# Gated MLP of a hybrid encoder: down-projection operands in rolling groups, token sums on VectorE

## The chip, the core and the metric

The kernel runs on one core of one Trainium2 chip. The metric is device time in microseconds (us) of one execution, and the median of several is quoted. The core's engines each work off their own instruction queue in order: PE (TensorE, with its weight loads, PEld, beside it), DVE (VectorE), ACT (ScalarE), POOL (GpSimd) and SP (SyncE), which here issues the transfers. Semaphores tie them together.

## The reference, cut to what matters

The model is an encoder of two layers on 1024 tokens and 1024 features. Every layer ends in the gated MLP, and the change touches only this:

```python
def _conv_ffn(x, norm_g, w_up, conv_w, conv_b, w_down):
    h = _rmsnorm(x, norm_g)
    up = h @ w_up
    gate, val = up[..., :D_FF], up[..., D_FF:]          # D_FF = 2816
    gate = conv(gate, conv_w) + conv_b                  # depthwise over tokens, width 3
    return (jax.nn.silu(gate) * val) @ w_down

def reference(x, ...):
    for layer in range(2):
        ...                                             # mixing: attention and retention, or gated linear attention
        x = x + _conv_ffn(x, ffn_norm[layer], ...)
    return x
```

Everything is float32. Below, `mid` is the input of the down projection, silu(gate) times val.

## The kernel before

Features lie on the partitions and tokens along the free axis, cut into two halves of 512. A float32 product is made of three matmuls (`mm3`, L350): each operand is split into a rounded high part, which ACT copies (L328), and the rest, which VectorE subtracts (L329). One matmul takes a 128x128 weight and 512 tokens.

**Up projection.** The 2816 features are 22 blocks of 128, i = 0 to 21. The first three go by plain products. Blocks 3 to 21 (`up_fast`) use a scheme of seven products in place of eight over two blocks of rows and the two token halves, each product 12 matmuls into one of four banks b1 to b4. The weights of a block come in two raw pages of 512 KB. VectorE turns them into sums (L1240 to L1243, where L1242 and L1243 write back into the first raw page) and splits them into pages `w` and `wf`; it also adds the banks into u, r and v (L1257). `gated_mid` then makes the convolution taps (L1286), ACT the Silu (L1287), and VectorE two multiplications by v and r (L1289). The raw pages rotate, so that the weights of a block can only be loaded when the splits of the earlier one have read theirs.

**Token sums.** The down projection uses the same scheme over pairs of blocks, for the first 16 blocks (`PAIRED`). From a pair it needs seven operands: three are the halves as they are and four are differences. `Mid.add` makes the four at the end of every odd block, one after the other, on POOL (L1321). All seven go to DRAM; the differences are written at the next block's start (`flush`, L1326).

**Down projection.** `Down` goes over the 16 blocks in two windows of eight (four pairs) and, in each, over four pairs of output blocks m: eight visits of seven products of 12 matmuls. `operands(w, p)` (L1344) loads the two pages (512 KB each, L1352) of operand p of window w through three staging pages `pg` and one `st`, and splits them. All operands of window 0 are loaded while the last up block runs, which is called the seam here, and those of window 1 in visit 3, each after the product that uses the same operand of window 0 last. Weights come six products ahead (`LEAD`; `part`, L1366), with four sums per visit on POOL. Each of the seven results of a visit is added to its accumulator by VectorE (L1417). The six blocks that are not paired are loaded in visit 7 (`rest`) and multiplied plainly after it.

The order on each engine's queue is set by a scheduler from the program's dependences and the rooms of each tag; the transfers all stand in SP's one queue. Thus a load behind one that waits for its page waits too.

The down projection's loop is short:

```python
        for p, (ps, outs) in enumerate(((b1, [u]), (b2, [u]), (b1, [c11]), (b3, [c22]), (b4, [c22]), (b3, [c21]), (b4, [c12]))):
            s = 7 * v + p
            self.product(s, ps, p in (0, 1, 3, 4))
            ...
            self.part(s + LEAD)
            if last and not w:
                self.operands(1, p)
```

Of the kernel before, what the change touches and what calls it, by code (L numbers as in the profile page):

```python
# [17 lines left out]
P = 128  # L18
# [4 lines left out]
H2 = 512  # L23
# [6 lines left out]
PAIRED, WIN, LEAD = 16, 8, 6  # L30
# [37 lines left out]
class Encoder:  # L68
# [1063 lines left out]
    def ffn(self, layer, h, ws, scale, h_gain, xs, gain=None, ahead=None):  # L1132
# [5 lines left out]
        with ExitStack() as stack:  # L1138
# [3 lines left out]
            T = {n: self.pairs(f"h{n}") for n in range(1, 5)}  # L1142
            self.xrooms.pop().close()
            late = stack.enter_context(self.room("left", tt=4))
# [45 lines left out]
    def pairs(self, tag):  # L1190

        pages = [[self.page([P, 2, H2], F32R, tag) for _ in range(2)] for _ in range(2)]
        return [tuple(x[:, j % 2] for x in pages[j // 2]) for j in range(4)]
# [28 lines left out]
    def up_fast(self, layer, i, h, T, mid):  # L1222
# [44 lines left out]
        add(r, b4, r)  # L1267
        yield
# [6 lines left out]
    def gated_mid(self, layer, i, g, v, mid):  # L1275
# [17 lines left out]
class Mid:  # L1293
# [4 lines left out]
    def __init__(self, e):  # L1298
        self.e, self.last, self.late = e, [], []
        self.d = [[[e.waiting() for _ in range(2)] for _ in range(7)] for _ in range(PAIRED // WIN)]  # L1300

    def add(self, i, cv):
        e, nc = self.e, self.e.nc
        if i >= PAIRED:
            d = e.dp.tile([P, 2, H2], F32, name=e.nm("d"))
            nc.sync.dma_start(out=d.rearrange("p h f -> p (h f)"), in_=cv)
            self.last.append(d)
            return
        w, j = divmod(i // 2, WIN // 2)
# [20 lines left out]
class Down:  # L1330
# [4 lines left out]

    A11, S2, A12, S3, S1, A22, S4 = range(7)

    def __init__(self, e, layer, mid):
        self.e, self.nc, self.mid = e, e.nc, mid
        self.w = e.io["ffn_w_down"][layer].rearrange("(k p) f -> p k f", p=P)  # L1340
        self.visits = [(w, m) for w in range(PAIRED // WIN) for m in range(0, NK, 2)]
        self.b, self.parts, self.raw = [{}, {}], {}, {}

    def operands(self, w, p):  # L1344

        e, nc, n = self.e, self.nc, {1: 2, 3: 3, 4: 1, 5: 4}.get(p)
        out = e.pairs(f"h{n}") if n else [tuple(e.page([P, H2], F32R, "hx") for _ in range(2)) for _ in range(4)]
        self.b[w][p] = out
        for a, d in enumerate(self.mid.d[w][p]):
            self.n = getattr(self, "n", -1) + 1  # L1350
            two = e.page([P, 2, H2], tag="st" if self.n % 4 == 3 else "pg")
            nc.sync.dma_start(out=two, in_=d.rearrange("j p f -> p j f"))  # L1352
            if n:
                e.split(two, *(bass.AP(x.tensor, x.offset, [list(x.ap[0]), [H2, 2], [1, H2]]) for x in out[2 * a]))
            else:
                for j in range(2):
                    e.split(two[:, j], *out[2 * a + j])

    def weights(self, v):

        e, nc, (w, m) = self.e, self.nc, self.visits[v]
        wg, wv = (e.page([P, 2, WIN // 2, P], F32, "raw") for _ in range(2))
        for x, c in ((wg, m), (wv, m + 1)):
            src = self.w[:, blk(w, WIN), blk(c)].rearrange("p (j two) f -> p two j f", two=2)
# [8 lines left out]
    def part(self, s):  # L1373

        if s >= 7 * len(self.visits):
            return
# [4 lines left out]
        t = e.page([P, 2, WIN // 2, P], F32R, "wd" if p in (self.S1, self.A22) else "w")  # L1381
# [11 lines left out]
    def product(self, s, ps, first):  # L1393
        t, b = self.parts.pop(s), self.b[self.visits[s // 7][0]][s % 7]
        for j in range(WIN // 2):
            self.e.mm3(ps, (t[:, 0, j], t[:, 1, j]), b[j], first and j == 0, j == WIN // 2 - 1, not first)

    def visit(self, v):
        e, nc, (w, m) = self.e, self.nc, self.visits[v]
        last = m == NK - 2  # L1400
        for i in range(2):
            for hf in range(2):
                if not w:
                    nc.sync.dma_start(out=self.x[m + i][hf], in_=self.xs[2 * (m + i) + hf])
        (c11, c12), (c21, c22) = self.x[m], self.x[m + 1]
        if not w:
            self.u[m] = e.page([P, H2], tag="hx")
        u = self.u[m]
        b1, b2, b3, b4 = (e.bank() for _ in range(4))
        for p, (ps, outs) in enumerate(((b1, [u]), (b2, [u]), (b1, [c11]), (b3, [c22]), (b4, [c22]), (b3, [c21]), (b4, [c12]))):  # L1410
            s = 7 * v + p
            self.product(s, ps, p in (0, 1, 3, 4))
            for x in outs:
                if not w and p == 0:
                    nc.scalar.copy(x, ps)
                else:
                    nc.vector.tensor_tensor(x, ps, x, ALU.add)  # L1417
# [9 lines left out]
    def rest(self, k, n):

        e = self.e
        for k in (k, k + 1):  # L1430
            two = e.page([P, 2, H2], tag="st" if k % 4 == 3 else "pg")
            self.nc.sync.dma_start(out=two, in_=self.mid.last[k])
            parts = [e.page([P, 2, H2], F32R, f"h{n}") for _ in range(2)]
            e.split(two, *parts)
            self.b[1][7 + k] = parts

    def run(self, xs, gain, ahead, stack, ends):
# [10 lines left out]
        for v in range(len(self.visits)):  # L1448
            self.visit(v)
# [241 lines left out]
```

## Time and profile before

| | before |
|---|---|
| median of 3 runs | 2611.17 us (2609.48 to 2611.77) |
| the profiled execution, its own time | 2607.8 us |
| its span in the trace | 2605.7 us |
| mean granted clock of PE | 0.994 |
| busy: PE, VectorE, ACT, POOL | 2511.6, 1811.3, 1202.1, 370.4 us |
| up blocks 4 to 15 by the fast scheme, layer 0 and layer 1 | 878.99 to 1120.69 and 2029.87 to 2277.24 us |
| seam, visits 0 and 1, layer 0 and layer 1 | 1158.77 to 1228.50 and 2339.95 to 2403.09 us |
| last part of visit 1 to visit 4, layer 0 and layer 1 | 1228.50 to 1299.77 and 2403.09 to 2471.99 us |

Times in the trace are counted from the span's start. The windows are cut at starts of products, so that the number of products in them is known from the program: 12 blocks of seven products each in the up windows; 21 and 19 products in the seam's, 23 in each of the last two. The count of matmuls in such a row can be a little short, since a few records are missing. In a row of a timeline, the brackets tell how long the engine was idle ahead of it and what ended this.

### The profile page before, as it was taken

The numbers are of one execution on the slowest core, as the hardware profiler recorded it, in microseconds if no ns is written. First come the engines' busy times: TensorE is split into PE (matmuls) and PEld (weight loads), VectorE is DVE, ScalarE is ACT, GpSimd is POOL, SyncE is SP. The second block draws the span as 40 slices with busy tenths as digits, with TensorE's granted clock in tenths as the row PEclk, the third lists the DMA queues.
The fourth block names the chain that finished last, engine by engine and source line by source line (L and its number), as shares of the span: only waits on it lengthen the run. The fifth ranks groups of instructions, "written<-read, shape, count | busy, mean of one in ns | idle before, by whom it ended". The sixth has DMA issues, their size and how long they took to land. (4 is left out here: it accounts for less than half of the span.)

```text
span 2605.7 us, 33289 instructions
## 1 busy us (share of the span) xinstructions
PE 2511.6 (96%) x12584; PEld 2091.0 (80%) x12584; DVE 1811.3 (70%) x2763; ACT 1202.1 (46%) x2215; POOL 370.4 (14%) x342
## 2 busy tenths in 40 slices
PE   8999999999999999998999999999999999998999
PEld 8989877777887877786788898887787777787787
DVE  6545788788578777777757545658687777777752
ACT  5234767779343333334434455566443333334422
POOL 0000033432001111103330000000001111102330
PEclk9999999999999999999999999999999999999999
DMA  5111100004622233337524121224722222337523
GB/s 192 46 38 42 50 26 9 13 14 154 193 89 89 93 97 101 102 114 236 162 83 134 57 64 42 73 69 133 236 80 97 85 97 97 102 105 250 162 75 120
DMA packets 305686, 262.21 MB, mean 101 GB/s; under 512 B 15788, under 2 KB 240149, under 8 KB 305525
## 3 DMA queue, kind: packets, MB, share of 16 engines
q1 hardware_dynamic: 300917, 251.69, 30.4%
q10 hardware_dynamic: 4608, 8.39, 0.9%
q8 instruction: 99, 1.62, 0.3%
q14 instruction: 62, 0.51, 0.1%
HBM read 189.52 MB, written 70.52 MB: 100 GB/s over the span
## 5 line engine op out<-in xcount | busy, mean ns | idle before, releaser
L350 PE MATMUL mm<-hx,w 128*128 128x512 f32 (+1 forms) x3408 | 828.2, 394 | 11.1 <-ACT wd L328 4.4
L350 PEld LDWEIGHTS mm<-hx,w 128*128 128x128 f32 (+1 forms) x3408 | 635.3, 188 | 150.2 <-ACT hx L1259 3.6
L328 ACT CAST w<-raw 128x512 fp32r<-128x512 f32 (+2 forms) x321 | 255.6, 807 | 449.7 <-PE mm L350 217.6
L329 DVE TENSOR_TENSOR w<-raw,w 128x1024 fp32r<-128x1024 f32 (+2 forms) x271 | 268.1, 994 | 260.8 <-ACT w L328 245.2
L350 PE MATMUL mm<-h,wf 128*128 128x512 f32 x1368 | 339.1, 397 | 29.7 <-DVE hx L1257 24.2
L350 PE MATMUL mm<-w,hx 128*128 128x256 f32 (+1 forms) x2304 | 364.1, 305 | 2.4 <-POOL w L329 1.9
L350 PE MATMUL mm<-h,w 128*128 128x512 f32 x1416 | 336.6, 390 | 0.0
L350 PEld LDWEIGHTS mm<-h,wf 128*128 128x128 f32 x1368 | 259.1, 191 | 94.9 <-DVE hx L1257 34.8
L350 PEld LDWEIGHTS mm<-w,hx 128*128 128x128 f32 x2304 | 307.7, 192 | 21.5 <-POOL w L329 2.9
L350 PEld LDWEIGHTS mm<-h,w 128*128 128x128 f32 x1416 | 264.7, 188 | 54.7
L328 ACT CAST wf<-raw 128x1024 fp32r<-128x1024 f32 x78 | 81.8, 1052 | 186.5 <-DVE raw L1243 173.4
L1321 POOL TENSOR_TENSOR tt<-pg 128x512 f32<-128x512 f32 x16 | 28.2, 1761 | 958.9 <-DVE pg L1289 734.9
L1257 DVE TENSOR_TENSOR hx<-mm,hx 128x512 f32<-128x512 f32 x190 | 129.8, 683 | 13.3 <-PE mm L350 13.3
L350 PE MATMUL mm<-hx,wf 128*128 128x512 f32 x552 | 133.5, 392 | 3.6 <-DVE hx L1257 3.6
L350 PEld LDWEIGHTS mm<-hx,wf 128*128 128x128 f32 x552 | 102.8, 188 | 29.2 <-DVE hx L1257 7.9
L329 DVE TENSOR_TENSOR wf<-raw,wf 128x1024 fp32r<-128x1024 f32 x78 | 95.2, 1222 | 23.8 <-ACT wf L328 23.8
L350 PE MATMUL mm<-h,wd 128*128 128x512 f32 x384 | 95.0, 401 | 12.1 <-DVE xa L1417 6.2
L350 PE MATMUL mm<-hr,hr 128*128 128x512 f32 x336 | 104.2, 404 | 1.4 <-ACT hf L1614 1.4
L350 PEld LDWEIGHTS mm<-h,wd 128*128 128x128 f32 x384 | 73.5, 193 | 30.3 <-issue 8.9
L1287 ACT ACTIVATE pg<-pg 128x1024 f32<-128x1024 f32 x44 | 46.7, 1061 | 107.0 <-DVE pg L1286 106.8
L1286 DVE SCALAR_TENSOR_TENSOR pg<-mm,c,pg 128x512 f32<-128x512 f32 (+1 forms) x100 | 74.1, 748 | 31.1 <-issue 16.9
L1321 POOL TENSOR_TENSOR tt<-pg,tt 128x512 f32<-128x512 f32 x32 | 52.2, 1632 | 293.2 <-DVE pg L1289 293.2
(385 smaller groups left out, 3621.8 us busy)
## 6 DMA issues: line engine op xcount, KB each, us to landing
raw<-in_ffn_w_up SPq DMA_DIRECT2D x88, 512.0 KB
pg<-d SPq DMA_DIRECT2D x52, 512.0 KB
d<-tt SPq DMA_DIRECT2D x64, 256.0 KB
raw<-in_ffn_w_down SPq DMA_DIRECT2D x64, 256.0 KB
d<-pg SPq DMA_DIRECT2D x55, 256.0 KB
raw<-in_ffn_w_down SPq DMA_DIRECT2D x32, 384.0 KB
raw<-in_w_in_odd SPq DMA_DIRECT2D x24, 512.0 KB
raw<-in_w_out_even SPq DMA_DIRECT2D x16, 512.0 KB
```

The source lines that it names most:

```text
L328: self.nc.scalar.copy(hi, src)
L329: return (rest or self.nc.vector).tensor_tensor(lo, src, hi.bitcast(F32), ALU.subtract)
L350: mm = lambda w, x, start, stop: self.nc.tensor.matmul(out, lhsT=w, rhs=x, start=start, stop=stop, skip_group_check=more)
L1257: add = lambda out, x, y: nc.vector.tensor_tensor(out, x, y, ALU.add)
L1286: nc.vector.scalar_tensor_tensor(dst, g[hf][:, src], cw(tap), dst, ALU.mult, ALU.add)
L1287: nc.scalar.activation(cv, cv, AF.Silu)
L1321: nc.gpsimd.tensor_tensor(t, x, y, ALU.subtract)
```

## The change

Three things are changed. The two windows of the down projection become four groups of four blocks (two pairs), of which two are live at a time. The visits are listed as (m, first group, number of groups): the first and the last visit use one group (products of 6 matmuls), the seven between them two (12 matmuls). Group 0 is loaded at the seam, group 1 in visit 0, group 2 in visit 3, group 3 in visit 4; the unpaired blocks in visits 7 and 8. The token sums move from POOL to VectorE and out of `Mid.add`: they are put on a list, and `Mid.step` makes one, called after the second r accumulation and after the Silu of each block. The pages `tt` for them become six in place of four and are closed one block later.

```diff
-PAIRED, WIN, LEAD = 16, 8, 6
+PAIRED, LEAD = 16, 6
+VISITS = [(0, 0, 1), (2, 0, 2), (4, 0, 2), (6, 0, 2), (0, 1, 2), (2, 2, 2), (4, 2, 2), (6, 2, 2), (0, 3, 1)]
...
-            late = stack.enter_context(self.room("left", tt=4))
+            late = stack.enter_context(self.room("left", tt=6))
...
-                    if i == PAIRED:
+                    if i == PAIRED + 1:
+                        while mid.todo:
+                            mid.step()
                         mid.flush()
...
         add(r, b4, r)
+        mid.step()
         yield
...
         nc.scalar.activation(cv, cv, AF.Silu)
+        mid.step()
         for hf, sl in enumerate(halves()):
             nc.vector.tensor_tensor(cv[:, sl], cv[:, sl], v[hf], ALU.mult)
...
-            self.first = two
+            self.first, self.t1 = two, t()
             nc.sync.dma_start(out=at(0), in_=two[0])
+            self.todo.append((self.t1, two[1], two[0], at(4)))
             return
...
-        for t, x, y in ((t1, b12, b11), (t2, b22, t1), (t3, b22, b12), (t4, b21, t2)):
-            nc.gpsimd.tensor_tensor(t, x, y, ALU.subtract)
-        self.late += [(at(p), t) for p, t in ((4, t1), (1, t2), (3, t3), (5, t4))]
+        self.todo += [(t(), two[1], b12, at(3)), (t2, two[1], t1, at(1)), (t(), two[0], t2, at(5))]
+
+    def step(self):
+
+        if self.todo:
+            t, x, y, d = self.todo.pop(0)
+            self.e.nc.vector.tensor_tensor(t, x, y, ALU.subtract)
+            self.late.append((d, t))
...
+    def stage(self, src):
+
+        self.loads += 1
+        two = self.e.page([P, 2, H2], tag="pg" if self.loads % 4 else "st")
+        self.nc.sync.dma_start(out=two, in_=src)
+        return two
+
+    def operands(self, g, p):
+
+        e, n = self.e, {1: 2, 3: 3, 4: 1, 5: 4}.get(p)
+        two = self.stage(self.mid.d[g][p].rearrange("j p f -> p j f"))
...
-        e, nc, (w, m) = self.e, self.nc, self.visits[v]
-        wg, wv = (e.page([P, 2, WIN // 2, P], F32, "raw") for _ in range(2))
+        e, nc, (m, g, n) = self.e, self.nc, VISITS[v]
+        wg, wv = (e.page([P, 2, 2 * n, P], F32, "raw") for _ in range(2))
...
-        for j in range(WIN // 2):
-            self.e.mm3(ps, (t[:, 0, j], t[:, 1, j]), b[j], first and j == 0, j == WIN // 2 - 1, not first)
+        bs = [b for i in range(n) for b in self.b[g + i, s % 7]]
+        for j, b in enumerate(bs):
+            self.e.mm3(ps, (t[:, 0, j], t[:, 1, j]), b, first and j == 0, j == 2 * n - 1, not first)
...
-            if last and not w:
-                self.operands(1, p)
-            if last and w and p in (1, 3, 4):
-                self.rest({1: 0, 3: 2, 4: 4}[p], {1: 2, 3: 3, 4: 1}[p])
+            then = {0: 1, 3: 2, 4: 3}.get(v)
+            if then:
+                self.operands(then, p)
+            if v in (7, 8) and p in (1, 3, 4):
+                self.rest({1: 0, 3: 1, 4: 2}[p] + 3 * (v - 7), {1: 2, 3: 3, 4: 1}[p])
```

VectorE's queue in layer 0, in the block that follows an odd paired block. L1257 (L1260 in the changed program) adds a bank into r, u or v; L1242 and L1243 (L1245 and L1246) write the raw weight page. Before:

```order
L1241 TENSOR_TENSOR raw_8767<-raw_8766,raw_8767 128x512
L329 TENSOR_TENSOR w_8791<-sw_8774,w_8791 128x512
L1257 TENSOR_TENSOR hx_8654<-mm_8651,hx_8653 128x512
L1242 TENSOR_TENSOR raw_8766<-sw_8774,raw_8766 128x512
L1243 TENSOR_TENSOR raw_8766<-raw_8766 128x512
L1257 TENSOR_TENSOR hx_8654<-mm_8652,hx_8654 128x512
L329 TENSOR_TENSOR wf_8784<-raw_8766,wf_8783 128x1024
L1257 TENSOR_TENSOR hx_8655<-mm_8651,hx_8653 128x512
```

The same stretch in the changed program, where L1331 is a token sum:

```order
L1244 TENSOR_TENSOR raw_8763<-raw_8762,raw_8763 128x512
L330 TENSOR_TENSOR w_8785<-sw_8768,w_8785 128x512
L1260 TENSOR_TENSOR hx_8653<-mm_8650,hx_8652 128x512
L1245 TENSOR_TENSOR raw_8762<-sw_8768,raw_8762 128x512
L1331 TENSOR_TENSOR tt_8708<-pg_8694,pg_8557 128x512
L1246 TENSOR_TENSOR raw_8762<-raw_8762 128x512
L1331 TENSOR_TENSOR tt_8705<-pg_8694,tt_8568 128x512
L1260 TENSOR_TENSOR hx_8653<-mm_8651,hx_8653 128x512
L330 TENSOR_TENSOR wf_8778<-raw_8762,wf_8777 128x1024
L1331 TENSOR_TENSOR tt_8709<-pg_8694,tt_8705 128x512
L1260 TENSOR_TENSOR hx_8654<-mm_8650,hx_8652 128x512
```

Three sums of the pair stand here, two of them ahead of the second r accumulation; the fourth, tt_8568, stands between L1245 and L1246 of the block before.

SP's queue at the seam of layer 0. d_7718 to d_7731 are the operands in DRAM: before, d_7718 + 2p and the next hold operand p of window 0; the store into d_10771 is that of up block 20. Before:

```order
L1352 DMA pg_10787<-d_7719 128x2x512
L1366 DMA raw_10900<-in_ffn_w_down 128x4x128 x2
L1366 DMA raw_10901<-in_ffn_w_down 128x4x128 x2
L1352 DMA pg_10848<-d_7720 128x2x512
L1352 DMA pg_10864<-d_7722 128x2x512
L1352 DMA pg_10870<-d_7723 128x2x512
L1306 DMA d_10771<-pg_10761 128x1024
L1352 DMA st_10884<-d_7725 128x2x512
L1352 DMA pg_10880<-d_7724 128x2x512
L1352 DMA pg_10892<-d_7726 128x2x512
L1352 DMA pg_10896<-d_7727 128x2x512
```

The same place in the changed program, where d_7718 + p holds operand p of group 0 and d_7725 + p that of group 1:

```order
L1358 DMA pg_10834<-d_7719 128x2x512
L1387 DMA raw_10862<-in_ffn_w_down 128x2x128 x2
L1387 DMA raw_10863<-in_ffn_w_down 128x2x128 x2
L1358 DMA pg_10840<-d_7720 128x2x512
L1358 DMA pg_10856<-d_7722 128x2x512
L1311 DMA d_10771<-pg_10761 128x1024
L1358 DMA st_10989<-d_7725 128x2x512
L1358 DMA pg_10930<-d_7723 128x2x512
L1358 DMA pg_10936<-d_7724 128x2x512
```

Operand 1 (S2), which was d_7720 behind the down weights, is now d_7719 ahead of them, and the first page of group 1 stands already among the pages of group 0.

SP's queue behind the weights of the next visit, in visit 0. The store into d_10928 is that of the last up block, 21 (that into d_10966 before); xa and xb are the accumulators. Before, the store comes behind all loads of window 0:

```order
L1366 DMA raw_11062<-in_ffn_w_down 128x4x128
L1352 DMA pg_10972<-d_7728 128x2x512
L1352 DMA st_10976<-d_7729 128x2x512
L1352 DMA pg_10988<-d_7730 128x2x512
L1366 DMA raw_11062<-in_ffn_w_down 128x4x128
L1366 DMA raw_11063<-in_ffn_w_down 128x4x128 x2
L1352 DMA pg_10994<-d_7731 128x2x512
L1404 DMA xb_11012<-d_7082 128x512
L1306 DMA d_10966<-pg_10956 128x1024
```

In the changed program:

```order
L1387 DMA raw_11006<-in_ffn_w_down 128x4x128
L1387 DMA raw_11007<-in_ffn_w_down 128x4x128 x2
L1358 DMA pg_11020<-d_7726 128x2x512
L1358 DMA pg_11036<-d_7727 128x2x512
L1311 DMA d_10928<-pg_10918 128x1024
L1426 DMA xb_10958<-d_7082 128x512
L1358 DMA st_11073<-d_7729 128x2x512
L1358 DMA pg_11057<-d_7728 128x2x512
L1358 DMA pg_11089<-d_7730 128x2x512
L1358 DMA pg_11105<-d_7731 128x2x512
```

The last four loads of group 1 stand behind the store of the last up block and one accumulator load.

## Rows read from the trace of the kernel before

**Rows 1.** The page's first part: busy time, share of the span, instructions.
```profile
PE 2511.6 (96%) x12584; PEld 2091.0 (80%) x12584; DVE 1811.3 (70%) x2763; ACT 1202.1 (46%) x2215; POOL 370.4 (14%) x342
```

**Rows 2.** Waits of PE; columns: us in total, times, longest us.
```profile
PE mm L350 <- DVE hx L1257: 27.9, 28, 4.1
```

**Rows 3.** Timeline of PE, blocks without sums: start us, us, what, idle before.
```profile
1120.69 2.88 PE L350 MATMUL mm<-h,wf 128*128 128x512 f32 x12
...
1139.73 1.07 PE L350 MATMUL mm<-h,wf 128*128 128x512 f32 x4
```

**Rows 4.** Timeline of PE: the same product in two blocks with sums, two blocks apart.
```profile
899.18 3.01 PE L350 MATMUL mm<-h,wf 128*128 128x512 f32 x12 [0.97 <-DVE hx L1257]
...
939.55 3.02 PE L350 MATMUL mm<-h,wf 128*128 128x512 f32 x12 [0.85 <-DVE hx L1257]
```

**Rows 5.** Timeline of DVE in a block that follows an odd one.
```profile
916.21 1.78 DVE L329 TENSOR_TENSOR w<-sw,w 128x512 fp32r<-128x512 f32 x1
...
918.52 1.17 DVE L1242 TENSOR_TENSOR raw<-sw,raw 128x512 f32<-128x512 f32 x1
919.72 1.67 DVE L1243 TENSOR_TENSOR raw<-raw 128x512 f32<-128x512 f32 x1
```

**Rows 6.** Timeline of POOL in the same stretch, the first of three.
```profile
915.93 1.52 POOL L1321 TENSOR_TENSOR tt<-pg,tt 128x512 f32<-128x512 f32 x1 [17.95 <-DVE pg L1289]
```

**Rows 7.** Timeline of DVE in two blocks without sums.
```profile
1136.81 0.69 DVE L329 TENSOR_TENSOR w<-sw,w 128x512 fp32r<-128x512 f32 x1
1137.41 0.69 DVE L1257 TENSOR_TENSOR hx<-mm,hx 128x512 f32<-128x512 f32 x1
...
1155.67 0.68 DVE L1257 TENSOR_TENSOR hx<-mm,hx 128x512 f32<-128x512 f32 x1
```

**Rows 8.** Windows: us, busy PE, PEld, DVE, ACT, POOL, PEclk, DMA, GB/s.
```profile
878.99:1120.69 241.70, 233.36 (x1010) 187.92 (x1008) 184.22 (x230) 79.59 (x96) 34.01 (x21) 1.00 0.31 99
2029.87:2277.24 247.37, 234.81 (x1010) 189.01 (x1009) 185.21 (x229) 79.64 (x96) 37.49 (x23) 0.99 0.30 98
1158.77:1228.50 69.73, 61.27 (x253) 49.37 (x252) 55.17 (x71) 33.73 (x50) 19.47 (x12) 0.95 0.73 242
1228.50:1299.77 71.27, 65.35 (x278) 52.62 (x276) 50.32 (x64) 29.02 (x45) 22.09 (x15) 0.98 0.50 161
2339.95:2403.09 63.14, 55.73 (x230) 44.86 (x228) 53.03 (x69) 30.19 (x47) 17.72 (x12) 0.95 0.77 253
2403.09:2471.99 68.90, 63.74 (x278) 51.49 (x276) 50.11 (x64) 29.02 (x45) 20.46 (x15) 1.00 0.49 159
```

**Rows 9.** Timelines of DVE and PE at the first fast block.
```profile
786.10 1.78 DVE L329 TENSOR_TENSOR h<-pp,h 128x512 fp32r<-128x512 f32 x1
...
809.35 0.73 PE L350 MATMUL mm<-h,wf 128*128 128x512 f32 x2 [2.55 <-ACT wf L328]
```

**Rows 10.** Timelines of DVE and PE at the seam and in visit 0.
```profile
1173.48 1.91 DVE L329 TENSOR_TENSOR h<-pg,h 128x1024 fp32r<-128x1024 f32 x1 [1.10 <-ACT h L328]
1175.32 3.42 DVE L1289 TENSOR_TENSOR pg<-pg,hx 128x512 f32<-128x512 f32 x2
...
1179.40 4.60 PE L350 MATMUL mm<-h,wf 128*128 128x512 f32 x12 [4.15 <-DVE hx L1257]
...
1203.19 3.41 PE L350 MATMUL mm<-h,wd 128*128 128x512 f32 x9 [2.83 <-DVE xa L1417]
```

**Rows 11.** Timeline of DVE in visit 3, operand splits with and without POOL's work.
```profile
1257.10 2.31 DVE L329 TENSOR_TENSOR h<-pg,h 128x1024 fp32r<-128x1024 f32 x1
...
1262.23 1.21 DVE L329 TENSOR_TENSOR h<-pg,h 128x1024 fp32r<-128x1024 f32 x1
```

**Rows 12.** Timeline of ACT: the cast of a block's weights, layer 0 and layer 1.
```profile
1145.54 1.05 ACT L328 CAST w<-raw 128x1024 fp32r<-128x1024 f32 x1 [2.06 <-DMA raw<-in_ffn_w_up]
...
2266.32 1.05 ACT L328 CAST w<-raw 128x1024 fp32r<-128x1024 f32 x1 [6.21 <-DMA raw<-in_ffn_w_up]
```

**Rows 13.** Chain that ended last, from 2350 to 2366 us: start us, us, what.
```profile
2356.99 6.54 DMA pg<-d
```

More of the change, by code (lines that the diff above doesn't have):

```diff
@@ L1140, in ffn @@
                 h4 = stack.enter_context(self.room("left", **{f"h{n}": 4}))
-            T = {n: self.pairs(f"h{n}") for n in range(1, 5)}
+            T = {n: [tuple(x[:, j] for x in two) for two in (self.pairs(f"h{n}"), self.pairs(f"h{n}")) for j in range(2)]
+                 for n in range(1, 5)}
             self.xrooms.pop().close()
-            late = stack.enter_context(self.room("left", tt=4))
+            late = stack.enter_context(self.room("left", tt=6))
             with self.room("right", pp=2, wf=2):
@@ L1190, in pairs @@
     def pairs(self, tag):
-        pages = [[self.page([P, 2, H2], F32R, tag) for _ in range(2)] for _ in range(2)]
-        return [tuple(x[:, j % 2] for x in pages[j // 2]) for j in range(4)]
+        return [self.page([P, 2, H2], F32R, tag) for _ in range(2)]
     def block_sums(self, h, j, out):
@@ L1298, in __init__ @@
     def __init__(self, e):
-        self.e, self.last, self.late = e, [], []
-        self.d = [[[e.waiting() for _ in range(2)] for _ in range(7)] for _ in range(PAIRED // WIN)]
+        self.e, self.last, self.todo, self.late = e, [], [], []
+        self.d = [[e.waiting() for _ in range(7)] for _ in range(PAIRED // 4)]
     def add(self, i, cv):
@@ L1340, in __init__ @@
         self.w = e.io["ffn_w_down"][layer].rearrange("(k p) f -> p k f", p=P)
[L1341 to L1357, printed above, removed]
+        self.b, self.parts, self.raw, self.loads = {}, {}, {}, 0
@@ new lines, in stage @@
+    def stage(self, src):
[6 more added lines that the diff above has]
+        two = self.stage(self.mid.d[g][p].rearrange("j p f -> p j f"))
+        if n:
+            pages = e.pairs(f"h{n}")
+            e.split(two, *pages)
+            self.b[g, p] = [tuple(x[:, j] for x in pages) for j in range(2)]
+        else:
+            self.b[g, p] = [tuple(e.page([P, H2], F32R, "hx") for _ in range(2)) for _ in range(2)]
+            for j in range(2):
+                e.split(two[:, j], *self.b[g, p][j])
@@ L1359, in weights, with rest @@
+    def rest(self, k, n):
+        two = self.stage(self.mid.last[k])
+        self.b[k] = self.e.pairs(f"h{n}")
+        self.e.split(two, *self.b[k])
     def weights(self, v):
[L1361 to L1362 removed]
+        e, nc, (m, g, n) = self.e, self.nc, VISITS[v]
+        wg, wv = (e.page([P, 2, 2 * n, P], F32, "raw") for _ in range(2))
         for x, c in ((wg, m), (wv, m + 1)):
[L1364 removed]
+            src = self.w[:, 4 * g:4 * (g + n), blk(c)].rearrange("p (j two) f -> p two j f", two=2)
@@ L1365, in weights @@
             for i in range(2):
                 nc.sync.dma_start(out=x[:, i], in_=src[:, i])
-        s1, s4 = (e.page([P, WIN // 2, P], tag="hx") for _ in range(2))
+        s1, s4 = (e.page([P, 2 * n, P], tag="hx") for _ in range(2))
         nc.gpsimd.tensor_tensor(s1, wv[:, 0], wv[:, 1], ALU.add)
@@ L1398, in visit @@
     def visit(self, v):
[L1399 to L1403, printed above, removed]
+        e, nc, (m, g, n) = self.e, self.nc, VISITS[v]
+        first, last = m not in self.u, g + n == PAIRED // 4
+        if first:
+            for i in range(2):
+                for hf in range(2):
                     nc.sync.dma_start(out=self.x[m + i][hf], in_=self.xs[2 * (m + i) + hf])
-        (c11, c12), (c21, c22) = self.x[m], self.x[m + 1]
@@ L1423, in visit @@
-        if w:
+            if first and p == 0:
+                nc.scalar.copy(x, ps)
+            else:
+                nc.vector.tensor_tensor(x, ps, x, ALU.add)
+            self.part(s + LEAD)
+            then = {0: 1, 3: 2, 4: 3}.get(v)
[3 more added lines that the diff above has]
+                self.rest({1: 0, 3: 1, 4: 2}[p] + 3 * (v - 7), {1: 2, 3: 3, 4: 1}[p])
+        if last:
             for x in (c21, c12, c22):
@@ L1425, in visit @@
                 nc.gpsimd.tensor_tensor(x, x, u, ALU.add)
[L1427 to L1435, printed above, removed]
     def run(self, xs, gain, ahead, stack, ends):
@@ L1447, in run @@
             self.x = [[e.page([P, H2], tag="xt") for _ in range(2)] for _ in range(NK)]
-        for v in range(len(self.visits)):
+        for v in range(len(VISITS)):
             self.visit(v)
```

29 lines of the change are left out of this document (11 added, 18 removed).

## The prediction

> **What bounds the kernel now.** The page's busy shares come first [rows 1]: PE is busy 96% of the span, so time can only come out of the stretches where it waits or runs slowly. The waits of PE come second [rows 2]: the largest entry by far is its wait for VectorE's line L1257, the accumulation of an up block. The third reading is the timeline of PE in two up blocks. A block without sums runs seven products of 12 matmuls, and the A22 products of two such blocks start 19.04 us apart [rows 3], which is 2.72 us per product with no gap. Two blocks with sums take 939.55 − 899.18 = 40.37 us, 2.29 more than 38.08, and both rows name L1257 [rows 4]. The fourth reading is VectorE beside POOL there: a VectorE operation of 128x512 takes 0.69 us in a block without sums [rows 7], but 1.78, 1.17 and 1.67 us where POOL's three subtractions of L1321 run (the first from 915.93 to 917.45) [rows 5, 6]. So POOL's operation makes VectorE's wait, 1.09 + 0.48 + 0.98 = 2.55 us per odd block.
>
> The Trainium skill, "SBUF — State Buffer", section "Who interferes with whom", calls VectorE's second port pair a lock shared with GpSimd, which a VectorE instruction with two SBUF inputs contends for; w<-sw has two such inputs, and its 1.78 us agrees.
>
> VectorE is not full (184.22 of 241.70 us [rows 8]), but it closes a loop: the first r accumulation, L1242, L1243, the split that frees the raw page, the next weights' load, their split, the taps, the multiplications, and the next r accumulation. Without POOL this loop takes 1155.67 − 1137.41 = 18.26 us [rows 7], 0.78 shorter than PE's 19.04; POOL's waits make it longer than PE's time, and PE waits.
>
> The windows [rows 8] give what is lost in all, as elapsed time less products times 2.72: the twelve paired fast blocks of each layer lose 241.70 − 228.48 = 13.2 and 247.37 − 228.48 = 18.9 us (32.1 together). The seam with the first two visits loses 69.73 − 21 × 2.72 = 12.6 and 63.14 − 19 × 2.72 = 11.5 us (24.1). The four-visit window's change loses 71.27 − 23 × 2.72 = 8.7 and 68.90 − 62.56 = 6.3 us (15.0).
>
> **The change part by part.** Matmuls stay the same (8 visits of 84 become 7 of 84 and 2 of 42), as do the loaded operand bytes.
>
> A, the sums in the paired blocks. Removed: 64 subtractions of POOL. Added: 64 of VectorE, 0.60 us each in a row of operations (1136.81 to 1137.41; the 0.69 in the row overlaps the next [rows 7]). By the order, one sum stands in the block after an even one and three in the block after an odd one, although the change asks for two per block. At most three of the four lie in the loop where nothing covers them; one stands where VectorE waits for ACT's cast. A pair then takes 2 × 18.26 + 3 × 0.60 = 38.32 us of loop against PE's 38.08: 0.24 short, 1.4 us over six pairs, or 0.84 and 5.0 us with all four in the loop. The loop starts ahead, so part of this never reaches PE. What stays besides are late weight loads in layer 1: ACT waited 6.21 us for one against 2.06 in an undisturbed block [rows 12], 4.15 late. The 32.1 us leave between 0 and 2 × 5.0 + 4.15 = 14; I take 5, near three sums per pair with part of the lead gone. **−27**, between −32 and −18.
>
> B, the start of the fast blocks. PE waits 2.55 us there for a split weight, and VectorE's splits beside POOL's subtractions take 1.78 instead of 0.69 us [rows 9]. Four such delays (4 × 1.09 = 4.4 us) lie ahead of it in each layer, and three sums (3 × 0.60 = 1.8) come in. 2.5 per layer: **−5**, between 0 and −8.
>
> C, the seam and visits 0 and 1. PE waits 4.15 us at the seam, runs the next 12 matmuls in 4.60 instead of 2.88 us (the stretch's granted clock is 0.95, part of it at the 1.2 GHz level), and waits 2.83 us in visit 0 for an accumulation [rows 10]. Ahead of the seam stand a split of 1.91 us that first waited 1.10 for its page, and two multiplications of 3.42 us [rows 10] beside POOL's work on the down weights. The first group needs half as many operand splits (one of 1.21 less, −1.2); visit 0's POOL operations have half the size, which takes up to 3.42 − 2 × 0.69 = 2.0 and 1.91 − 1.21 = 0.7; and the waited-for load stands ahead of the down weights in SP's order (−1.1). That is up to 5.0 per layer, and with it the slow matmuls (1.7).
> Against this stands the second group, which is loaded in visit 0. That visit is only 7 × 1.36 = 9.5 us long (half of 19.04). VectorE needs 7 × (0.60 for the eviction + 0.60 for the weight + 1.21 for the operand) = 16.9 us there, 7.4 more; but the last of it is wanted in the second half of visit 1's products, 2.72 us apart, and the same seven operands were split in this stretch before. On SP, four of the group's loads stand behind the last store of an up block, which waits for the multiplications, and behind the accumulator loads. Ends: −24 (everything lost here goes) and +15 (7.4 paid in full in both layers). I take 5 + 1.7 less about 3 of lateness per layer, which is nearest to the seam's own rows: **−7**.
>
> D, the change of window. Before, one visit loads and splits 14 pages: 7 × 1.20 + 14 × 1.21 = 25.3 us of VectorE in 19.04 us of PE. After, visits 3 and 4 take seven each: 16.9 us, which fits. POOL's weight subtractions still slow some splits (2.31 against 1.21 [rows 11]), about three per visit, so each visit stands at 16.9 + 3 × 1.10 = 20.2 and can lose 1.2, 2 × 2 × 1.2 = 4.8 in all, and a restart may come with it; of the 15.0 I take **−9**; ends −15 and 0.
>
> E, the ninth visit. Visit 8's products last 1.36 us, about one eviction (0.68) and its handover; seven more evictions per layer. Where VectorE is idle they cost nothing; paid in full, 2 × 7 × 0.68 = 9.5. I take **+1.5**. The weight loads are more and smaller with the same bytes, in stretches where DMA is at most 0.77 busy [rows 8]: zero, up to 2.
>
> Sum against the profiled execution's own 2607.8 us: −27 − 5 − 7 − 9 + 1.5 = −46.5, 2561.3 us. The median of the runs lies 3.4 above that execution, so **2565 us**.
>
> **The rivals.** (1) Partial: all four sums pace the loop and loads come late (A −18, its end, instead of −27), and the second group eats the seam's gain (C 0 instead of −7): 16 worse, 2581 us. For it: the loop has only 0.78 us to spare per block. Against: it has a lead at the start, and one sum stands in a wait.
> (2) Better: every wait named in A to D goes but 3 of A and half of C's: −29 − 8 − 12 − 15 = −64, 2547 us. For it: the unpaired blocks show a PE without gaps. Against: POOL still works in the visits.
> (3) Slower, by one mechanism: the second group's loads go one at a time. A load took 6.54 us from issue to landing on the chain that ended last [rows 13]; with the cast and split of 1.05 + 1.21 that is 8.8 us, seven of them 61.6, and from the last up block's start to the end of visit 0 there are 19.04 + 9.5 = 28.5. PE would wait 33 us per layer: 2607.8 − 27 − 5 − 9 + 1.5 + 66 = 2634, a median of 2638 us. It decides against the change from about 20 us of waiting per layer, one page every 7 us. For it: the loads stand in one in-order queue behind a store that waits. Against: four staging pages can be in flight, and this stretch moves 242 GB/s [rows 8], 2.2 us per 512 KB.
> (4) VectorE saturates: a pair keeps its 40.37 us and the four sums come on top, 4 × 0.60 = 2.4 us per pair, 14 pairs: +34 instead of −27 and B's −5, 2607.8 + 34 − 7 − 9 + 1.5 = 2627, a median of 2631 us. For it: VectorE is the engine that PE waits for. Against: it is busy only 76% of this stretch [rows 8], and the waits for POOL leave it with its work.
> The Trainium skill, "Perfetto Trace Analysis", section "Optimizing Scalar/DVE Operations", says that a saturated VectorE may be relieved by giving work to GpSimd, and that the shared port can spoil this; by its first half this change goes the wrong way and case 4 holds, by its second half A holds. The slowed rows [rows 5] bear out the second.
>
> **How the numbers follow.** Forecast 0.68 (its own range is 2553 to 2577: C's 7 gone and one more of A's or D's moved by 5, either way), partial 0.13, better 0.09, loads one at a time 0.05, VectorE saturated 0.02; the remaining 0.03 lie within 0.2% of no change, about 5 us, which is what a measurement of this kernel can tell from none. The range from 2546 to 2590 holds the first three, less a tail. Faster 0.90, same 0.03, slower 0.07.
>
> **What would show it.** In the changed trace L1245's and L1246's operations should take 0.69 us in every paired block, POOL be idle there, and pairs take 38.1 to 38.5 us. The stretch of twelve blocks should last about 231 us in each layer. The seam should show PE waiting under 3 us, and visits 3 and 4 about 20 us each. The forecast is wrong if PE waits more than 5 us at one place in visit 1 (case 3), or if a pair takes over 39 us without any slowed operation (case 4).

## The result, and the profile after

The changed kernel takes 2572.04 us (2567.66 to 2572.68) against 2610.32 us before: a ratio of 0.985, interval 0.9832 to 0.9867, so it is 38 us faster. The forecast was 2565 us, its range 2546 to 2590. The profiled execution took 2571.87 us, with a span of 2570.0.

The windows of the changed kernel, cut at the same kinds of products as in [rows 8] (us, busy PE, PEld, DVE, ACT, POOL, PEclk, DMA, GB/s). The first two are the twelve up blocks, the third and fifth the seam to the sixth product of visit 1, the fourth and sixth four visits, from the last product of visit 1 to that of visit 5:

```profile
877.25:1105.73 228.48, 228.48 (x1009) 189.25 (x1008) 178.38 (x250) 81.61 (x96) 0.00 (x0) 1.00 0.32 105
2009.84:2239.14 229.30, 229.30 (x1010) 188.77 (x1008) 176.46 (x252) 79.55 (x96) 0.00 (x0) 1.00 0.33 107
1143.81:1198.36 54.55, 50.56 (x213) 40.69 (x212) 47.47 (x66) 30.40 (x46) 15.40 (x11) 0.97 0.74 235
1198.36:1288.69 90.33, 80.44 (x335) 64.53 (x334) 58.31 (x79) 33.61 (x54) 25.97 (x19) 0.96 0.52 167
2301.83:2350.77 48.94, 44.47 (x190) 34.74 (x188) 42.55 (x63) 26.00 (x41) 12.64 (x10) 1.00 0.78 259
2350.77:2440.45 89.68, 80.41 (x336) 64.60 (x334) 58.84 (x80) 33.61 (x54) 27.61 (x20) 0.96 0.52 167
```

Twelve blocks last 228.48 us, to the hundredth what 84 products take without a gap, and VectorE is no busier than before (178.38 against 184.22 us) although it does 20 operations more: the waits for POOL were in that busy time. The four visits hold 28 products, 76.2 us, and last 90.33 and 89.68: there 14.2 and 13.5 us are lost, where the change of window lost 8.7 and 6.3 before. Step by step, in us and in both layers together:

| step | forecast | measured | from |
|---|---|---|---|
| A, up blocks | −27 | −31.3 | 241.70 and 247.37 to 228.48 and 229.30 |
| B, start of the fast blocks | −5 | −7.8 | PE loses 1.6 and 1.5 us, before 4.7 and 6.2 |
| C, seam, visits 0 and 1 | −7 | −10.4 | 54.55 − 17.5 × 2.72 = 6.9 and 48.94 − 15.5 × 2.72 = 6.8, before 12.6 and 11.5 |
| D, visits 2 to 5 | −9 | +12.7 | 14.2 and 13.5 over 28 products each, before 8.7 and 6.3 over 23 |
| E, ninth visit | +1.5 | about 0 | no wait of PE there |

This makes −37; the profiled executions differ by −35.9.

PE's timeline of the changed kernel, the start of the fast blocks and, in layer 0, the longest wait of each of the visits 2 to 5 (in visit 2 with the S1 product ahead of it; a visit's seven products are A11, S2, A12, S3, S1, A22 and S4, in this order):

```profile
809.57 2.79 PE L351 MATMUL mm<-h,wf 128*128 128x512 f32 x11 [0.34 <-DVE wf L330]
...
1211.58 2.88 PE L351 MATMUL mm<-h,wd 128*128 128x512 f32 x12
1218.75 4.62 PE L351 MATMUL mm<-h,wd 128*128 128x512 f32 x12 [4.29 <-DVE xa L1436]
...
1241.74 4.32 PE L351 MATMUL mm<-h,wd 128*128 128x512 f32 x12 [2.04 <-DVE xa L1436]
...
1264.20 3.00 PE L351 MATMUL mm<-h,wd 128*128 128x512 f32 x12 [1.47 <-DVE xa L1436]
...
1285.89 2.97 PE L351 MATMUL mm<-h,wd 128*128 128x512 f32 x12 [1.33 <-DVE xa L1436]
```

The 2.55 us of [rows 9] are 0.34. In each of these visits the A22 product waits for an eviction, that is, for VectorE to add the bank of an earlier product to its accumulator. Visit 2 waits longest, and VectorE splits no operands there (none from 1192.68 to 1229.99 us), so operand splits cannot be the reason. What VectorE did there stands in four timelines of the changed kernel around 1210 us (VectorE, ACT, POOL, and SP, which issues the weight load of visit 3):

```profile
1205.50 0.69 DVE L330 TENSOR_TENSOR w<-raw,w 128x512 fp32r<-128x512 f32 x1 [0.79 <-ACT w L329]
1214.48 1.22 DVE L330 TENSOR_TENSOR w<-raw,w 128x512 fp32r<-128x512 f32 x1 [8.29 <-PE mm L351]
1215.62 0.68 DVE L1436 TENSOR_TENSOR hx<-mm,hx 128x512 f32<-128x512 f32 x1
...
1218.02 0.68 DVE L1436 TENSOR_TENSOR xa<-mm,xa 128x512 f32<-128x512 f32 x1
...
1213.83 1.66 ACT L329 CAST w<-raw 128x512 fp32r<-128x512 f32 x3 [7.87 <-POOL raw L1406]
...
1209.77 1.29 POOL L1389 TENSOR_TENSOR hx<-raw 128x512 f32<-128x512 f32 x1 [9.22 <-DMA raw<-in_ffn_w_down]
1211.14 1.29 POOL L1390 TENSOR_TENSOR raw<-raw,raw 128x512 f32<-128x512 f32 x1
1212.50 1.29 POOL L1406 TENSOR_TENSOR raw<-hx,raw 128x512 f32<-128x512 f32 x1
...
1204.13 0.92 SPq L1387 DMA_DIRECT2D raw<-in_ffn_w_down  x2
```

VectorE stands idle for 8.29 us, with evictions queued; the one that A22 needs begins at 1218.02. Its next operation is a weight split of the *next* visit; the split waits for ACT's cast, the cast for POOL's third sum, POOL for the load, and the load was issued only at 1204.13, when the raw page came free. The row puts VectorE's wait down to PE, but the split needs the cast, and ACT's first cast, begun at 1213.83, is what came last. This is theory W (weights) of the expectations below.

### The profile page after: what moved, and what is told of

It reads as the page before. It is cut to its first block, busy times and chain, and to the rows that moved or that the text cites. A ratio compares the mean times of both kernels' runs of the same rounds, so it can differ in the third digit from the quotient of the medians.

```text
span 2570.0 us, 33323 instructions
## 1 busy us (share of the span) xinstructions
PE 2501.4 (97%) x12584; PEld 2090.5 (81%) x12584; DVE 1793.7 (70%) x2855; ACT 1207.7 (47%) x2229; POOL 264.5 (10%) x286
## 4 chain that ended last, share of the span: by engine, by line
PE 74%; DVE 13%; ACT 5%; DMA 4%; issue 3%; POOL 1%; SPq 0%; POOLq 0%; DVEq 0%; ACTq 0%
PE mm L351 64%; DVE w L330 1%; DVE h L330 1%; ACT w L329 1%; DMA raw<-in_ffn_w_down 1%; PE mr L1104 1%; PE mr L351 1%; PE mr L1541 1%; DVE sr L1597 1%; PE mr L1543 1%; DVE pg L1290 1%; DVE hx L330 1%; PE mr L854 1%; PE mr L1034 1%; PE mr L1596 1%
## 5 line engine op out<-in xcount | busy, mean ns | idle before, releaser
L329 ACT CAST w<-raw 128x512 fp32r<-128x512 f32 (+3 forms) x329 | 257.3, 792 | 421.6 <-PE mm L351 214.2
L330 DVE TENSOR_TENSOR w<-raw,w 128x1024 fp32r<-128x1024 f32 (+3 forms) x279 | 272.3, 980 | 225.9 <-ACT w L329 202.2
L351 PE MATMUL mm<-h,wf 128*128 128x512 f32 x1368 | 329.2, 389 | 0.6 <-DVE wf L330 0.6
L351 PEld LDWEIGHTS mm<-w,hx 128*128 128x128 f32 x2304 | 307.7, 192 | 21.9 <-POOL w L330 3.0
L1389 POOL TENSOR_TENSOR hx<-raw 128x512 f32<-128x512 f32 (+1 forms) x18 | 22.7, 1263 | 1666.2 <-DMA raw<-in_ffn_w_down 1630.2
L1260 DVE TENSOR_TENSOR hx<-mm,hx 128x512 f32<-128x512 f32 x190 | 129.9, 684 | 42.8 <-PE mm L351 42.8
L351 PE MATMUL mm<-h,wd 128*128 128x512 f32 x384 | 99.8, 411 | 17.8 <-DVE xa L1436 9.1
L330 DVE TENSOR_TENSOR wf<-raw,wf 128x1024 fp32r<-128x1024 f32 x78 | 95.4, 1223 | 17.3 <-ACT wf L329 17.3
L351 PE MATMUL mm<-hf,w 128*128 128x512 f32 x384 | 88.8, 392 | 0.0
```

Source lines behind the costliest of these rows:

```text
L329: self.nc.scalar.copy(hi, src)
L330: return (rest or self.nc.vector).tensor_tensor(lo, src, hi.bitcast(F32), ALU.subtract)
L351: mm = lambda w, x, start, stop: self.nc.tensor.matmul(out, lhsT=w, rhs=x, start=start, stop=stop, skip_group_check=more)
L1260: add = lambda out, x, y: nc.vector.tensor_tensor(out, x, y, ALU.add)
```

## Experiments

Ratios are to the kernel before, timed on the same chip in the same session (median 2605.5 to 2606.3 us there).

**e1, the sums alone.** The changed `Mid` and its calls, in the kernel before; windows and visits as they were:

```diff
...
         add(r, b4, r)
+        mid.step()
         yield
...
```

> The kernel before with the token sums on VectorE alone (six tt pages, one sum per step); the down projection keeps its two windows and eight visits. Theory W (weights): the waits of PE in the visits come from the next visit's weights, whose load, POOL sums, cast and split stand ahead of evictions in VectorE's queue, and the operand groups do not touch them; the whole gain is the sums'. Then this kernel lies at 2568 to 2574 us, not slower than the changed kernel (2572), with the up phase free of waits and about 39 us of losses left in seam and visits, as before (21.3 and 17.8 us in the two layers). Theory G (groups help, sums hurt): the rolling groups gain about 14 us in the visits, as predicted, and the moved sums cost as much there; then this kernel lies at 2583 to 2588 us.

Measured: 2568.09 us, ratio 0.9855 (0.984 to 0.9869). From the seam on PE loses 17.3 and 19.9 us in the two layers, where the kernel before lost 21.3 and 17.8. Theory W; G falls. The edit changes two things at once, the engine of the sums and their place (one by one instead of four in a row); which of them gains was not tried apart. The slowed rows [rows 5] and the 0.68 us of the same lines now speak for the engine.

**e2, the groups alone.** The changed kernel with the sums back on POOL:

```diff
...
-        self.todo += [(t(), two[1], b12, at(3)), (t2, two[1], t1, at(1)), (t(), two[0], t2, at(5))]
+        for t, x, y in ((t1, b12, b11), (t2, b22, t1), (t3, b22, b12), (t4, b21, t2)):
+            nc.gpsimd.tensor_tensor(t, x, y, ALU.subtract)
...
```

> The changed kernel with the token sums back on POOL, all four at the end of the odd block, and four tt pages: the rolling groups and nine visits alone. Theory W: nothing is gained, 2609 to 2615 us; the up phase loses its 32 us as before, and seam and visits lose 39 to 42 us. Theory G: 2594 to 2599 us, with under 28 us lost in seam and visits.

Measured: 2607.34 us, ratio 1.0006 (0.9997 to 1.0015). The rolling groups and the nine visits by themselves change nothing in the time. With e1 this puts the whole gain on the sums. But the groups move where PE loses. The windows of this kernel, cut like the last four of the changed kernel's (17.5 and 28 products in layer 0, 15.5 and 28 in layer 1):

```profile
1159.70:1214.99 55.29, 51.09 (x213) 40.58 (x212) 48.90 (x67) 30.43 (x46) 14.79 (x11) 0.97 0.74 247
1214.99:1304.95 89.96, 80.90 (x336) 65.32 (x334) 57.97 (x78) 33.69 (x54) 24.50 (x19) 0.94 0.51 162
2338.43:2388.60 50.17, 44.49 (x190) 34.77 (x188) 44.87 (x64) 26.48 (x42) 14.65 (x11) 1.00 0.77 260
2388.60:2478.00 89.40, 80.88 (x336) 65.55 (x334) 57.96 (x78) 33.71 (x54) 24.36 (x19) 0.94 0.50 163
```

At the seam 7.7 and 8.0 us are lost instead of 12.6 and 11.5, and in the four visits behind it 13.8 and 13.2 instead of 8.7 and 6.3. e1, without the groups, loses 9.8 and 12.1 at the seam and 7.6 and 7.8 behind it.

**e3, weight sums on VectorE.** All four of a visit:

```diff
-        nc.gpsimd.tensor_tensor(s1, wv[:, 0], wv[:, 1], ALU.add)
-        nc.gpsimd.tensor_tensor(wv[:, 0], wg[:, 0], wv[:, 0], ALU.subtract)
+        nc.vector.tensor_tensor(s1, wv[:, 0], wv[:, 1], ALU.add)
+        nc.vector.tensor_tensor(wv[:, 0], wg[:, 0], wv[:, 0], ALU.subtract)
...
-            nc.gpsimd.tensor_tensor(r[p], r[self.S1], r[p], ALU.subtract)
+            nc.vector.tensor_tensor(r[p], r[self.S1], r[p], ALU.subtract)
...
-            nc.gpsimd.tensor_tensor(r[self.S4], r[p], r[self.S2], ALU.subtract)
+            nc.vector.tensor_tensor(r[self.S4], r[p], r[self.S2], ALU.subtract)
```

> The changed kernel with the four weight sums of every visit on VectorE instead of POOL. Theory W: three of POOL's sums (1.29 us each or more, one after the other) stand between the landing of a visit's weights and the cast that VectorE's queue waits for; on VectorE they take 0.6 us each and no longer slow its other operations, so the waits ahead of A22 products in visits 2 to 5 (4.29, 2.04, 1.47, 1.33 us in layer 0) shrink by some 2 us each, and restarts at the lower clock go: 2556 to 2563 us. Theory O (VectorE is overloaded by operand splits in visits 0, 3 and 4): VectorE gets 4 x 0.6 = 2.4 us more per visit and the waits grow there: 2574 to 2585 us.

Measured: 2545.99 us, ratio 0.977 (0.9758 to 0.9783), beyond what W had said. VectorE's timeline of this kernel in visit 2, and PE's from the last product of visit 1 to that of visit 5:

```profile
1204.43 0.69 DVE L1436 TENSOR_TENSOR hx<-mm,hx 128x512 f32<-128x512 f32 x1 [0.34 <-PE mm L351]
1207.76 0.69 DVE L1389 TENSOR_TENSOR hx<-raw 128x512 f32<-128x512 f32 x1 [2.65 <-DMA raw<-in_ffn_w_down]
...
1209.10 0.68 DVE L1436 TENSOR_TENSOR xb<-mm,xb 128x512 f32<-128x512 f32 x1
1209.70 0.68 DVE L1406 TENSOR_TENSOR raw<-hx,raw 128x512 f32<-128x512 f32 x1
...
1211.13 1.29 DVE L330 TENSOR_TENSOR w<-raw,w 128x512 fp32r<-128x512 f32 x2
1212.34 0.69 DVE L1436 TENSOR_TENSOR xa<-mm,xa 128x512 f32<-128x512 f32 x1
...
1196.52 5.15 PE L351 MATMUL mm<-hx,w 128*128 128x512 f32 x22
...
1209.67 2.88 PE L351 MATMUL mm<-h,wd 128*128 128x512 f32 x12
1213.08 3.03 PE L351 MATMUL mm<-h,wd 128*128 128x512 f32 x12 [0.53 <-DVE xa L1436]
...
1273.16 5.60 PE L351 MATMUL mm<-hx,w 128*128 128x512 f32 x24
```

From the first sum to the split pass 3.37 us (1207.76 to 1211.13) instead of 4.71 (1209.77 to 1214.48). The edit changes the order of VectorE's queue as well: two evictions (1204.43 and 1209.10) now stand ahead of the split, and the one that A22 needs begins 1.21 us after the split's start (1212.34) where it was 3.54 (1218.02). So the shorter chain gives 1.34 us and the order 2.33. The four visits last 76.64 us, 0.5 over their products; in the changed kernel they lost 14.2. VectorE got 2.4 us more work per visit and made PE wait less: theory O falls.

**e4, a third raw page.** Taken from the staging, which keeps three:

```diff
-                        late = stack.enter_context(self.room("left", st=1, wd=2))
+                        late = stack.enter_context(self.room("left", rawd=1, wd=2))
...
-        two = self.e.page([P, 2, H2], tag="pg" if self.loads % 4 else "st")
+        two = self.e.page([P, 2, H2], tag="pg")
...
-        wg, wv = (e.page([P, 2, 2 * n, P], F32, "raw") for _ in range(2))
+        wg, wv = (e.page([P, 2, 2 * n, P], F32, "raw" if (2 * v + k) % 3 else "rawd") for k in range(2))
```

> The changed kernel with three raw pages for the weights of the visits in place of two; the page comes from the staging, which has three pages in place of four. Theory W: a visit's weight load no longer waits for the split of the last weight of the visit before (1203.43, with the load issued at 1204.13), so it lands some us earlier, and the waits in visits 2 and 5, where no operands are loaded, fall under 1 us; in all 2558 to 2568 us. Theory O: the weight load is not what is late; fewer staging pages make the operand visits worse: 2573 to 2590 us, and the wait of 4.29 us in visit 2 stays.

Measured: 2549.15 us, ratio 0.9783 (0.9769 to 0.9797), again beyond W. POOL keeps its sums, but begins earlier (POOL and PE timelines of this kernel, the weights of visit 3 and the wait in visit 2):

```profile
1204.32 1.28 POOL L1389 TENSOR_TENSOR hx<-raw 128x512 f32<-128x512 f32 x1 [5.14 <-DMA raw<-in_ffn_w_down]
...
1209.08 2.88 PE L351 MATMUL mm<-h,wd 128*128 128x512 f32 x12
1213.29 3.02 PE L351 MATMUL mm<-h,wd 128*128 128x512 f32 x12 [1.33 <-DVE xa L1436]
```

Counted from the start of the S1 product (1209.08 here, 1211.58 in the changed kernel), the first sum begins 2.95 us sooner and the A22 product 2.96 us sooner, with VectorE's order unchanged from the split on: the wait follows the landing one for one. PE waits 1.33 in place of 4.29 us, not quite under the 1 us that W had said; in layer 1 a wait of 3.21 stays in visit 2, whose reason is open. From seam to last visit PE loses 26 us in both layers instead of 41. e4 moves the landing alone, e3 shortens the chain behind it and changes VectorE's order too; e4 is thus the one that shows the chain by itself, and e3 agrees. Why the load lands late is partly open: it is issued when its raw page comes free, but SP issues four operand loads right behind it (1205.10 to 1207.69 in the changed kernel), and what these take from it was not tried.

**e6, each token sum made twice.**

```diff
-            self.e.nc.vector.tensor_tensor(t, x, y, ALU.subtract)
+            for _ in range(2):
+                self.e.nc.vector.tensor_tensor(t, x, y, ALU.subtract)
```

> The changed kernel with every token sum made twice, so 64 more VectorE operations of 0.60 us in the up phase. Theory L (the loop of the weights decides): three of a pair's four doublings lie in the loop, which took 18.81 + 19.33 = 38.14 us per pair against PE's 38.08; with 1.8 us more it takes 39.9, PE waits 1.9 us in every pair once the lead of some 3 us is used up, about 10 us per layer: some 18 to 24 us slower than the changed kernel, a ratio of about 0.992 to 0.995 to the kernel before. Theory F (VectorE has 71 us of idle time in 310 us of this phase, and work fits in there): 0 to 4 us slower, a ratio of 0.985 to 0.987.

Measured: 2576.68 us, ratio 0.9885 (0.9869 to 0.9901), between the two. The trace decides: the blocks keep their 19.04 us, so L falls; in the profiled execution (2580.32 us) some 6 us went to the start of the fast blocks, where more sums precede the first weights, and about 2 to the visits. VectorE's timeline shows why (first the changed kernel in a block after an odd one, then this kernel in such a block):

```profile
1063.76 0.68 DVE L1245 TENSOR_TENSOR raw<-sw,raw 128x512 f32<-128x512 f32 x1
1064.36 0.68 DVE L1331 TENSOR_TENSOR tt<-pg,pg 128x512 f32<-128x512 f32 x1
1064.96 0.68 DVE L1246 TENSOR_TENSOR raw<-raw 128x512 f32<-128x512 f32 x1
1065.56 0.68 DVE L1331 TENSOR_TENSOR tt<-pg,tt 128x512 f32<-128x512 f32 x1
1066.17 0.68 DVE L1260 TENSOR_TENSOR hx<-mm,hx 128x512 f32<-128x512 f32 x1
1066.77 1.22 DVE L330 TENSOR_TENSOR wf<-raw,wf 128x1024 fp32r<-128x1024 f32 x1
1067.91 0.68 DVE L1331 TENSOR_TENSOR tt<-pg,tt 128x512 f32<-128x512 f32 x1
1070.57 0.69 DVE L1260 TENSOR_TENSOR hx<-mm,hx 128x512 f32<-128x512 f32 x1 [1.98 <-PE mm L351]
```

```profile
1029.86 0.68 DVE L1332 TENSOR_TENSOR tt<-pg,pg 128x512 f32<-128x512 f32 x1
1030.46 0.68 DVE L1246 TENSOR_TENSOR raw<-raw 128x512 f32<-128x512 f32 x1
1031.06 0.68 DVE L1332 TENSOR_TENSOR tt<-pg,pg 128x512 f32<-128x512 f32 x1
1031.66 0.68 DVE L1260 TENSOR_TENSOR hx<-mm,hx 128x512 f32<-128x512 f32 x1
1032.26 1.22 DVE L330 TENSOR_TENSOR wf<-raw,wf 128x1024 fp32r<-128x1024 f32 x1
1033.40 2.87 DVE L1332 TENSOR_TENSOR tt<-pg,tt 128x512 f32<-128x512 f32 x4
1036.65 0.69 DVE L1260 TENSOR_TENSOR hx<-mm,hx 128x512 f32<-128x512 f32 x1 [0.38 <-PE mm L351]
```

Only the sum ahead of L1246 lengthens the loop, and here too it is one: the scheduler put the doubles behind L1246, not where L had them. What a second sum ahead of L1246 would cost is therefore not shown. The next stands where the split waits for ACT's cast, and the last, four operations here, where the accumulation waits for PE anyway: 1.98 us there, 0.38 here.

**e7, windows with weight sums on VectorE.** e1 with e3's edit.

> The kernel before with the token sums on VectorE (as in e1) and the four weight sums of every visit on VectorE too (as in e3): two windows, eight visits. It tells what the rolling groups are worth once the weight chain is short. Theory H (groups help, but the weight chain hid it): visit 3 then has 14 operand splits, 25.3 us of VectorE with the 7 evictions and weight splits, and 2.4 us of weight sums, in 19.04 us of PE; PE waits 6 to 9 us per layer there, and about 4 more at the seam: 10 to 25 us slower than e3, a ratio of 0.981 to 0.987 to the kernel before. Theory N (the groups are worth nothing either way): as e3, 0.975 to 0.979.

Measured: 2552.5 us, ratio 0.9794 (0.9778 to 0.9811), where e3 has 0.977. The intervals overlap, and PE's losses from seam to last visit are nearly alike (19.7 us in both layers, 18.0 in e3): nearer to N. The splits of the 14 operand pages do not fall into visit 3 alone: they run from 1235.53 to 1265.88 us, through visits 3 and 4. PE's largest wait in this stretch is the A22 product of visit 4 (0.66 in layer 1):

```profile
1268.34 3.02 PE L350 MATMUL mm<-h,wd 128*128 128x512 f32 x12 [0.64 <-DVE xa L1427]
```

**e8, both edits of e3 and e4.**

> The changed kernel with both edits of e3 and e4: weight sums on VectorE, and three raw pages with three staging pages. Theory W: e3 lost about 18 us in both layers, nearly all of it in visits 0 and 1, where VectorE works without a pause and a third raw page adds nothing, while a staging page less may delay operands there: within 4 us of e3, a ratio of 0.975 to 0.979. If the weight load is still what is late in visits 0 and 1, another 6 to 10 us go: 0.973 or less.

Measured: 2547.7 us, ratio 0.9774 (0.9759 to 0.9788): like e3. One link made short is enough.

**e9, weight sums on VectorE in the kernel before.** Nothing else.

> The kernel before with one edit: the four weight sums of every visit on VectorE. Token sums stay on POOL, windows and visits stay. Theory W: the waits in the visits come from the weight chain whatever the operand groups, and the sums of the up phase have nothing to do with them; so this edit alone gains what it gained beside the token sums (e1 to e7, some 15 to 20 us): a ratio of 0.992 to 0.994, with the up phase losing its 32 us as before. Theory S (the chain is late only because VectorE enters the visits later or earlier after the moved sums): less than 8 us, 0.997 or more.

Measured: 2588.86 us, ratio 0.9936 (0.9919 to 0.9953), as W said. The up blocks still lose their time and seam and visits lose 24.7 instead of 39.1 us. With e1 the product is 0.9855 × 0.9936 = 0.9792; e7 has 0.9794: the two moves off POOL add up.

**e10, the changed kernel again.**

> The changed kernel as it is, on the same chip as its neighbours here: a ratio of 0.983 to 0.987, so that e1 (0.9855) can be told from it only if it lies at an end of that.

Measured: 2569.73 us, ratio 0.9867 (0.9853 to 0.9882). e1 cannot be told from it. In this profiled execution PE loses 37.7 us from seam to last visit, in that of the result 41.4: a few us between two such sums say nothing.

**e11, e3 with weights seven products ahead.**

```diff
-PAIRED, LEAD = 16, 6
+PAIRED, LEAD = 16, 7
```

> The kernel of e3 with weights prepared seven products ahead instead of six. What e3 still loses in seam and visits, 18 us in both layers, lies in visits 0 and 1. If it is the weights of visit 1 that come late there (theory W once more), one product's time more, 1.36 us in visit 0, takes 3 to 6 us of it: 0.975 or less. If VectorE's work is what fills that short visit (theory V: 16.9 us of work in 9.5 us), it changes nothing or hands the wait on: 0.976 to 0.980.

Measured: 2643.95 us, ratio 1.015 (1.0133 to 1.0167), which neither theory had. The waits of PE in this kernel lie elsewhere, in the mixing stage of the second layer, before its MLP:

```profile
PE mr L854 <- DVE hr L1018: 24.2, 5, 6.9
PE mr L1119 <- ACT hr L1113: 19.1, 8, 4.3
PE mr L1034 <- ACT hr L1021: 14.6, 6, 5.1
```

The changed kernel's first of these is 3.9 us. The constant seems to have moved the order of work there; how stays open. Seam and visits lose 19.7 us (18.0 in e3), so the time says nothing on them and the trace, within what e10 shows of such sums, speaks for V.

## Why the prediction held, and where it failed

**A** was right in its mechanism: without POOL's sums L1245 and L1246 take 0.68 us and the blocks run without a gap. The term mis-sized is what stays: 5 us by the forecast, 0.8 measured. I put three of a pair's four sums into the loop. In e6 the loop takes 18.84 and 18.82 us in blocks of six and of two sums (L1245 at 915.66, 934.50 and 953.32): what one sum makes of it, 18.26 + 0.60 = 18.86 us, and under PE's 19.04. In the changed kernel blocks of one and of three sums take 18.81 and 19.33 us (L1245 at 1044.95, 1063.76 and 1083.09). The 0.5 more matches the next weights' load, 4.34 us from its issue to ACT's cast (1068.02 to 1072.36) against 3.84 in e6 (919.93 to 923.77), and PE's lead covers it. Late loads came again in layer 1, where ACT waits for them up to 4.44 us; PE lost no more than the 0.8 us.

**B** was right, 3 us too small.

**C** went as forecast in sign and nearly in size, but it is no gain of its own. The groups alone bring the 24.1 us of this stretch to 15.7 (e2), the sums alone only to 21.9 (e1); and the same groups raise the loss of the visits behind it from 15.0 to 27.0 us (e2; 15.3 in e1). What C gained, D lost. That visit 0 is too short for its work is borne out so far: e3 and e8 lose nearly all that they still lose there. But e7, without a short visit, loses as much, so the short visit's own share stays open.

**D** is the step that failed. It took the window's loss for VectorE's overload, 25.3 us of work in a visit of 19.04, and it measured +12.7 us instead of −9. e7 has these splits, spread over two visits, and PE waits 0.66 us there at most; e2 spreads them further and gains nothing. The trace of the kernel before had shown it already, in the last wait of the window (timelines of ACT and PE, layer 0):

```profile
1289.42 1.66 ACT L328 CAST w<-raw 128x512 fp32r<-128x512 f32 x3 [5.93 <-POOL raw L1385]
...
1292.64 7.29 PE L350 MATMUL mm<-hx,w 128*128 128x512 f32 x24 [2.82 <-ACT wd L328]
```

ACT's cast waits for a weight sum of POOL, VectorE's split (1290.07) and an eviction (1291.82) come behind it, and PE waits 2.82 us and then runs 24 matmuls in 7.29 instead of 5.60 us: half of the 8.7 us lost there. I had priced each visit's work, but not the order in the queue: a split of the next visit's weights stands ahead of this visit's evictions, and what it waits for is a load, three sums of POOL and a cast. The forecast named POOL's slow-down of the splits and missed POOL's place in that chain. Why the chain is late in four visits of the changed kernel and in fewer before was not tried by itself; that group 1's loads and splits share SP's and VectorE's queues with the weights of visits 1 and 2 is my reading of the order, no more.

So the forecast was 7 us too low, and that it came so near is in part luck: A, B, C and E came out 12 us better than said and D 21.7 worse. Of its signs, the blocks' length and POOL's idleness came as said; a wait of 3.1 us in visit 0 lies just over the 3 us named, and visits 3 and 4 take 22.7 and 22.1 us instead of about 20 (S4 products at 1223.21, 1245.86 and 1267.95). The serial loads of rival 3 did not occur (PE's waits in visits 0 and 1 are 3.1 us at most), nor did rival 4. Of the rule cited from the Trainium skill, "Perfetto Trace Analysis", section "Optimizing Scalar/DVE Operations", the second half held, that work given to GpSimd may not help VectorE: its busy time in the up blocks fell from 184.22 to 178.38 us as it took the sums over.

The kernel of e3 beats both, at 2545.99 us.

## What to carry to other kernels

An engine that is idle and named as a releaser is not short of time: look at what its next instruction waits for, and at what is queued behind that. Moving small elementwise work off a slow helper engine can shorten two things at once, the neighbour's operations and a chain of dependences. Count added work by the waits it falls into, not by its sum. When a change gains at one place, look whether the next one pays for it.

## What was not expected of the hardware

POOL's weight sums of 128x512 took 1.29 us alone and up to 2.16 us beside VectorE, which makes the same sum in 0.69 (0.60 apart in a row). On this kernel the two moves off POOL, 64 token sums (e1) and 64 weight sums (e9), are worth 1.45% and 0.64% of the time, with PE doing the same products.
